# A hybrid decoder layer: block 0's load put into the written order, and a new order for 1200 steps around the change of token halves

## The chip, the core and the metric

The kernel runs on one core of a Trainium2 chip. The core has engines that work side by side, each through its own list of instructions in order: TensorE (PE) multiplies matrices, VectorE (DVE), ScalarE (ACT) and GpSimd (POOL) work element by element, and SyncE (SP) issues the transfers between the chip's memory (DRAM) and the core's on-chip memory. An instruction that waits holds up everything behind it on its engine. The metric is the time of one execution in microseconds (us), the median of several runs.

## The reference

One layer of a hybrid decoder over 2048 tokens of width 1024, in float32. Its first half mixes tokens along two paths (SSD and RWKV7); its second half is a gated feed-forward part with a short causal convolution:

```python
h = x + rms_norm(concat(ssd(xn @ w_in), rwkv7(xn @ w_in)) @ w_out)    # xn = rms_norm(x)
...
u = rms_norm(h) @ w_up                    # 2 x 2816 columns: a gate and a value
u = causal_dwconv(u, conv_w, conv_b)      # 3 taps along the tokens
y = h + rms_norm((silu(gate) * value) @ w_down)
```

## The kernel before, in words

**The whole.** The program has three stages, one after another with some overlap: phase_R (the RWKV path, 16 blocks of 128 tokens), phase_S (the SSD path and the output projection) and phase_F (the feed-forward part). Each float32 operand of a product is split into a high and a low half of 16 bits; the high half is made by ScalarE, the low half ("the value less its high half") by VectorE or GpSimd, and TensorE runs three products of halves instead of one.

**The order of the work.** The order on each engine is written, not found while the program runs. In phase_R a list of words, HEAD, names the steps of the first blocks: `R0.load/5` is step 5 of the load of block 0, `L.w.4/1` is step 1 of loading weight piece 4. A step runs once; a second call of the same step does nothing. HEAD stands under `tc.manual_schedule(engines=HANDS)`, where HANDS are VectorE, ScalarE, GpSimd and SyncE: what is emitted there stays in the order in which it is emitted, while instructions emitted outside are placed by the compiler's scheduler. Block 0's `load` (L845) is emitted ahead of that, at L1399. It reads the 128 token rows (xin), squares them (L870), takes mean and root on GpSimd (L874, L878), scales the rows (L889, ScalarE), makes the high half xh (L890, ScalarE) and the low half (L882, VectorE), has both transposed into xt by transfers (L892, L885), and stores xt in XN (L894). Beside it the weights are loaded: each piece wst (L788, SyncE) is split into wr by ScalarE (L791) and VectorE (L794). The products on L689 need xt and wr.

**The feed-forward part.** It works on two halves of 1024 tokens. In each half there are 22 up products, u_0_0 to u_0_21 and u_1_0 to u_1_21, each computed as seven half-size products (Strassen's scheme) of 12 matmuls, 128x512 outputs each. Their operands are seven combinations b0 to b6 of the tokens, split into halves, and seven combinations w0 to w6 of the weights. The b's of half 1 are built while half 0 ends: token rows hs come from DRAM, GpSimd subtracts (L2026), ScalarE makes the high half (L2051), VectorE or GpSimd the low one (L2056). An up product's results u leave their PSUM banks into C: the first is copied by ScalarE (L2223), the others are added by VectorE (L2227). Then come a scale (L2258), the taps (L2262), silu (L2272) and the gate (L2275), which leave p.

Two up products make a pair, whose p's are combined into seven factors fa (L2315, L2051, L2056). The down products run over two or three pairs: seven combinations dw0 to dw6 of the down weights, split like the b's (L2406, L2409), times fa0 to fa6 (L2445). Their results d are added to acc by ScalarE (L2456) and VectorE (L2458). The names count half, products and quarter: d_0_803 is half 0, the down product after pair 8, and so on.

In half 0 the weights are made on the core and stored in DRAM (UW at L2175, DW at L2414); in half 1 they are loaded back (w at L2147, dw at L2384). The buffers of dw are a ring of four tiles, two for each of dw0 to dw6, so the loads for one step are issued when the products two steps before it are through (dw4 takes the tiles of dw0). The last pair of half 0 (pair 10) is special: its weights are called dwx, in a ring of two tiles that lies where C0 was, and its rows r0, r1 and their difference rt lie where C1 and a1 were. When half 0 ends, Finish adds the norm and the residual and stores the rows (L2494, L2524, L2537, L2544).

**The planner.** phase_F doesn't emit its work at once: each operation is noted with an engine, an estimated time and what it reads and writes, and the class Program (run at L96) puts all of them into one list, todo, by due times worked out back from TensorE's list. The first 140 steps (OPENED) are mixed into the end of phase_S; the rest are emitted one by one under the manual schedule:

```python
todo = prog.run()
yield prog.entry + todo[:OPENED]
prog.on = None
with tc.manual_schedule(engines=HANDS):
    for step in todo[OPENED:]:
        step()
```

Of the kernel before, what the change touches and what calls it, by code (L numbers as in the profile page):

```python
# [389 lines left out]
OPENED = 140  # L390
# [227 lines left out]
""".split())  # L618


HANDS = {getattr(mybir.EngineType, x) for x in ("DVE", "Activation", "Pool", "SP")}


# [70 lines left out]
def phase_R(tc, K, const, tables, x, w_r, w_c, wl_d, g2_d, XN, XC, YR, iters=16):  # L694
    nc = tc.nc
    V, S, G_ = nc.vector, nc.scalar, nc.gpsimd
    with ExitStack() as ctx:
# [696 lines left out]
            return t.rearrange("p j (u s) -> p j u s", s=64)  # L1394

        blocks = [Block(it) for it in range(iters)]
        blocks[0].do("load")
        loads = Loads()
        K.hand.enter_context(tc.manual_schedule(engines=HANDS))  # L1399
        for step in HEAD.split():  # L1400
# [4 lines left out]
        for it in range(2, iters - 1):  # L1405
            for step in PLAN.split():
                step, _, part = step.partition("/")
                who, name, *a = step.split(".")
                n = it + {"n": 1, "f": 0, "b": -1, "a": -2}[who]
# [568 lines left out]
def phase_F(tc, K, w_u, w_d, H, HN, out, halves=2):  # L1978
# [6 lines left out]
    with ExitStack() as ctx:  # L1985
# [607 lines left out]
        for n, h in enumerate(hs):  # L2593
# [25 lines left out]
            if n + 1 < halves:  # L2619
# [2 lines left out]
                ups[n * NFF + NFF].weights()  # L2622
                fin = Finish(n)
        todo = prog.run()
        yield prog.entry + todo[:OPENED]
        prog.on = None
        with tc.manual_schedule(engines=HANDS):
            for step in todo[OPENED:]:
# [5 lines left out]
def hybrid_layer(ctx, tc, io, out):  # L2634
# [8 lines left out]
    with tc.manual_schedule(engines={mybir.EngineType.PE}):  # L2643
        cp = ExitStack()
        const = cp.enter_context(tc.tile_pool(name="const", bufs=1, side="left"))
        tables = [io[n] for n in ("cst", "par", "rows", "rows16")]
        K.hand = ExitStack()
        blocks, front, rest = phase_R(
            tc, K, const, tables, io["x"], io["w_r"], io["w_c"], io["wl"], io["g2"], XN, XC, YR)
        pairs, chunks, setup = phase_S(tc, K, io["x"], io["w_z"], io["w_dt"], io["w_o"], XN, XC, YR, Hd, HN)  # L2650
        F = phase_F(tc, K, io["w_u"], io["w_d"], Hd, HN, out)
        entry = next(F)
        K.hand.close()
# [117 lines left out]
```

## Time and profile before

| | |
|---|---|
| time before, median of 3 runs | 2493.3 us (2490.09 to 2493.72) |
| the profiled execution's own time | 2499.62 us |
| its span, from the first to the last instruction | 2497.8 us |
| granted TensorE clock, mean | 0.986 of full speed |
| busy: TensorE, VectorE, ScalarE, GpSimd | 2398.1, 1909.4, 1197.4, 1082.4 us |

The median comes from unprofiled runs and the rows from one profiled execution, which took 6.3 us more than the median. A row of a timeline gives the start, the duration, the engine, the line in kernel.py, the operation, the tile written and the tiles read, how many instructions the row joins, and in brackets how long the engine had stood idle ahead of it and what released it. PE is TensorE, DVE VectorE, ACT ScalarE, POOL GpSimd, SPq the queue of SyncE. Numbers of buffers are left out there, so `dwx<-r` can be any of the dwx tiles.

### The profile page before, as it was taken

The page shows a single profiled execution, that of the slowest core. Times are in us where ns is not written, and L with a number is a line of the kernel's source. Part 1 is how long each engine was busy: PE and PEld are TensorE (multiplying, and loading weights), DVE is VectorE, ACT ScalarE, POOL GpSimd, SP SyncE. Part 2 cuts the span into 40 slices and gives each one's busy share as a digit, 9 for nine tenths or more (in the row PEclk, how much of TensorE's full clock was granted, in tenths as well). Part 3 has the DMA queues.
Part 4 walks back from the last instruction along what each step waited for, and adds up shares of the span by engine and source line. Part 5 has one row for each costly group of instructions (what it writes and reads, how often), then busy time and mean ns, then how long its engine had stood idle before and what let it go on. Part 6 is the DMA issues. An engine that isn't in the chain of part 4 may idle for free. (4 is left out here: it accounts for less than half of the span.)

```text
span 2497.8 us, 53811 instructions
## 1 busy us (share of the span) xinstructions
PE 2398.1 (96%) x21210; PEld 1519.3 (61%) x21212; DVE 1909.4 (76%) x3790; ACT 1197.4 (48%) x2407; POOL 1082.4 (43%) x1134
## 2 busy tenths in 40 slices
PE   4999999999999899999988999999989999999998
PEld 4899999999999665555533444444434444444443
DVE  6878778877887567678999799999999735546557
ACT  7556665666566544444555545453443432313132
POOL 3334443444344522223334658585847522213135
PEclk9999999999999989999999999999999999999999
DMA  7432332233323536565775444445445533333253
GB/s 224 91 67 58 80 78 67 57 79 75 72 57 71 170 114 170 149 178 162 213 223 166 166 159 147 162 144 177 145 161 192 169 106 97 106 101 98 88 160 109
DMA packets 344412, 319.12 MB, mean 128 GB/s; under 512 B 203232, under 2 KB 248672, under 8 KB 340832
## 3 DMA queue, kind: packets, MB, share of 16 engines
q1 hardware_dynamic: 344016, 315.43, 43.1%
q8 instruction: 166, 2.72, 0.5%
q14 instruction: 86, 0.70, 0.1%
q10 hardware_dynamic: 144, 0.26, 0.0%
HBM read 187.85 MB, written 110.99 MB: 120 GB/s over the span
## 5 line engine op out<-in xcount | busy, mean ns | idle before, releaser
L2205 PE MATMUL u<-b,w 128*128 128x512 f16 x3696 | 809.5, 381 | 22.7 <-ACT C L2223 11.5
L2205 PEld LDWEIGHTS <-w 128*128 128x128 f16 x3696 | 363.2, 98 | 465.1 <-issue 34.5
L689 PE MATMUL d<-xt,wr 128*128 128x129 f16 x5376 | 333.7, 224 | 26.3 <-ACT wr L791 17.9
L689 PEld LDWEIGHTS <-wr 128*128 128x128 f16 x5376 | 319.1, 100 | 40.0 <-ACT wr L791 17.9
L2445 PE MATMUL d<-dw,fa 128*128 128x512 f16 x1512 | 333.6, 380 | 4.2 <-DMA dw<-DW 2.2
L2445 PEld LDWEIGHTS <-fa 128*128 128x128 f16 x1596 | 156.9, 98 | 205.1 <-issue 18.8
L2227 DVE TENSOR_TENSOR C<-u,C 128x512 f32<-128x512 f32 x220 | 150.7, 685 | 156.8 <-PE u L2205 151.3
L689 PE MATMUL c<-xt,wc 128*128 128x131 f16 x3072 | 195.1, 224 | 5.7 <-ACT tv L919 3.5
L689 PEld LDWEIGHTS <-wc 128*128 128x128 f16 x3072 | 183.2, 99 | 11.0 <-issue 7.3
L2458 DVE TENSOR_TENSOR acc<-d,acc 128x512 f32<-128x512 f32 x212 | 140.3, 684 | 54.2 <-PE d L2445 53.3
L2056 POOL TENSOR_TENSOR fa<-p,fa 128x512 f16<-128x512 f32 x100 | 140.7, 1421 | 50.1 <-ACT fa L2051 50.1
L2262 DVE SCALAR_TENSOR_TENSOR p<-C,fpar,p 128x1024 f32<-128x1024 f32 x88 | 124.5, 1415 | 34.5 <-ACT p L2258 34.4
L2058 DVE SCALAR_TENSOR_TENSOR w<-us,w 128x512 f16<-128x512 f32 x132 | 134.3, 1029 | 7.6 <-ACT w L2051 6.6
L968 DVE SCALAR_TENSOR_TENSOR ca<-c,cw,ca 128x128 f32<-128x128 f32 x360 | 114.5, 345 | 25.5 <-ACT ca L958 21.5
L2262 DVE SCALAR_TENSOR_TENSOR a<-C,fpar,a 128x1024 f32<-128x1024 f32 x88 | 125.0, 1420 | 3.7 <-ACT a L2258 2.4
L2223 ACT ACTIVATE C<-u 128x512 f32<-128x512 f32 x88 | 52.2, 593 | 156.9 <-PE u L2205 133.8
L1140 DVE TENSOR_TENSOR tmp<-atl,xl 128x60 f32<-128x60 f32 (+24 forms) x465 | 117.1, 252 | 11.5
L2051 ACT ACTIVATE fa<-p 128x512 f16<-128x512 f32 x110 | 65.4, 623 | 125.0 <-DVE p L2275 113.1
L1146 DVE TENSOR_TENSOR xl<-xl,tmp 128x60 f32<-128x60 f32 (+24 forms) x465 | 111.2, 239 | 13.9
L2051 ACT ACTIVATE w<-us 128x512 f16<-128x512 f32 x132 | 80.3, 624 | 85.6 <-PE u L2205 28.6
L2268 POOL COPY fcarry<-C 128x2 f32<-128x2 f32 x88 | 38.6, 440 | 160.8 <-DVE C L2227 160.7
L2178 POOL TENSOR_TENSOR us<-us,us 128x512 f32<-128x512 f32 x51 | 82.7, 1625 | 46.2 <-DVE w L2058 27.3
(334 smaller groups left out, 4326.3 us busy)
## 6 DMA issues: line engine op xcount, KB each, us to landing
UW<-w SPq DMA_DIRECT2D x154, 256.0 KB
w<-UW SPq DMA_DIRECT2D x154, 256.0 KB
us<-in_w_u_dram SPq DMA_DIRECT2D x88, 256.0 KB
DW<-dw SPq DMA_DIRECT2D x70, 256.0 KB
dw<-DW SPq DMA_DIRECT2D x56, 256.0 KB
hs<-HN SPq DMA_DIRECT2D x48, 256.0 KB
r<-in_w_d_dram SPq DMA_DIRECT2D x10, 1024.0 KB
xin<-in_x_dram SPq DMA_DIRECT2D x16, 512.0 KB
```

Of the source, the lines that this page charges most:

```text
L689: nc.tensor.matmul(ps, w[:, a, kt, :], xt[:, b, kt, cols], start=n == 0, stop=n == 3 * KT - 1)
L968: V.scalar_tensor_tensor(out=acc[:, q], in0=m["rc", e][:, q, k:k + 128], scalar=cw[:, e + q, k:k + 1], in1=acc[:, q], op0=ALU.mult, op1=AL ...
L1140: chain.tensor_tensor(out=self.tmp[:, :k, :n], in0=self.atl[:, j, j + 1:32].unsqueeze(1).to_broadcast([P, k, n]), in1=self.xl[:, :k, j:j + ...
L1146: chain.tensor_tensor(out=self.xl[:, :k, j + 1:32], in0=self.xl[:, :k, j + 1:32], in1=self.tmp[:, :k, :n], op=ALU.add)
L2051: S.activation(h, src, AF.Copy, **({} if scale is None else {"scale": scale}))
L2056: {"V": V, "G": G_}[engine].tensor_tensor(out=l, in0=src, in1=h, op=ALU.subtract)
L2058: V.scalar_tensor_tensor(out=l, in0=src, scalar=scale, in1=h, op0=ALU.mult, op1=ALU.subtract)
L2205: nc.tensor.matmul(bk[at], self.w[i][:, u, k, :], self.half.b[i][:, k, v, :], start=start and n == 0, stop=n == 11, skip_group_check=True)
L2227: op("V", .61, lambda: V.tensor_tensor(out=part(j, x), in0=bk[at], in1=part(*a), op=ALU.add), (("u", 4 * s + at), (*(c0, c1)[a[0]], a[1])) ...
L2262: V.scalar_tensor_tensor(out=o[j], in0=C[j][:, 2 - d:1026 - d], scalar=cw(g, 2 - d), in1=o[j], op0=ALU.mult, op1=ALU.add)
L2445: nc.tensor.matmul(bk[s, t], pairs[m].a[i][:, u, t * P:t * P + P], pairs[m].w[n][0][:, v, :], start=new and m == 0 and u == v == 0, stop=m ...
L2458: V.tensor_tensor(out=acc[j][:, t], in0=bk[s, t], in1=acc[j][:, t], op=ALU.add)
```

## The change

It has two parts. No instruction is added or taken away on any engine.

```diff
@@ -618,6 +618,52 @@
+TURN = 1000
+TURNED = """
+2 30 6 20 1 16 11 15 21 3 0 10 17 5 22 19 8 33 7 9 13 4 14 36 28 18 45 29 27 38 12 32 51 25 23 31 35 43 41 34 47 50 54
...
+1199
+"""
 HANDS = {getattr(mybir.EngineType, x) for x in ("DVE", "Activation", "Pool", "SP")}
@@ -1394,7 +1440,6 @@
         blocks = [Block(it) for it in range(iters)]
-        blocks[0].do("load")
         loads = Loads()
         K.hand.enter_context(tc.manual_schedule(engines=HANDS))
         for step in HEAD.split():
@@ -2622,6 +2667,8 @@
         todo = prog.run()
+        turn = [OPENED + TURN + int(n) for n in TURNED.split()]
+        todo[min(turn):max(turn) + 1] = [todo[n] for n in turn]
         yield prog.entry + todo[:OPENED]
```

First, block 0's load is no longer emitted ahead of the manual schedule. HEAD already names its steps (`R0.load/1` and so on), which until now found the step done; now each is emitted at the place where it stands in HEAD. Second, steps 1140 to 2339 of todo are put into the order of the table TURNED, a permutation of 1200 numbers. A step is moved by 20 places in the mean, by 285 at most. The steps are those of all five engines, so TensorE's order changes as well. On TensorE the stretch runs from u_0_15 of half 0 to u_1_6 of half 1; outside it and the first rows of the front the order on each engine is the same.

In the rows below, the line numbers of the changed kernel are 45 to 47 higher than before's for the same operation.

**At the end of half 0.** ScalarE, around the copy of u_0_210 (the first quarter of the last up product) into C_0_210, before:

```order
L2051 ACTIVATE b0_1_26325<-hs10100_26246 128x512
L2258 ACTIVATE p_0_20_26328<-C_0_200_26165,fpar_21402 128x1024
L2051 ACTIVATE w5_0_21_26348<-us_0_2101_26143 128x512
L2051 ACTIVATE b2_1_26372<-hs10110_26323 128x512
L2223 ACTIVATE C_0_210_26375<-u_0_210_26284 128x512
L2272 ACTIVATE p_0_20_26328<-p_0_20_26328 128x1024
L2051 ACTIVATE fa0_0_10_26399<-p_0_20_26328 128x512
L2223 ACTIVATE C_0_210_26375<-u_0_210_26284 128x512
```

and in the changed kernel:

```order
L2303 ACTIVATE p_0_20_26316<-C_0_200_26123,fpar_21402 128x1024
L2303 ACTIVATE a_0_20_26320<-C_0_201_26124,fpar_21402 128x1024
L2268 ACTIVATE C_0_210_26338<-u_0_210_26232 128x512
L2096 ACTIVATE b0_1_26348<-hs10100_26273 128x512
L2317 ACTIVATE p_0_20_26316<-p_0_20_26316 128x1024
L2096 ACTIVATE w5_0_21_26383<-us_0_2101_26154 128x512
L2096 ACTIVATE b0_1_26348<-hs10300_26277 128x512
L2268 ACTIVATE C_0_210_26338<-u_0_210_26232 128x512
```

The first copy (L2223, now L2268) stood behind the high halves of b0 (from hs10100) and b2 (from hs10110); it now stands ahead of b0, and that of b2 is no longer among these rows.

VectorE, around the low half of the first dwx (from r0, pair 10), before:

```order
L2262 SCALAR_TENSOR_TENSOR a_0_21_26468<-C_0_211_26376,fpar_21402,a_0_21_26468 128x1024
L2409 SCALAR_TENSOR_TENSOR dw4_0_8_26496<-r_0_8_25593,dw4_0_8_26496 128x512
L2275 TENSOR_TENSOR p_0_21_26446<-p_0_21_26446,a_0_21_26468 128x1024
L2409 SCALAR_TENSOR_TENSOR dw4_0_9_26498<-r_0_9_25622,dw4_0_9_26498 128x512
L2315 TENSOR_TENSOR p_0_20_26328<-p_0_20_26328,p_0_21_26446 128x512
L2056 TENSOR_TENSOR fa4_0_10_26517<-p_0_21_26446,fa4_0_10_26517 128x512
L2315 TENSOR_TENSOR p_0_20_26328<-p_0_20_26328 128x512
L2056 TENSOR_TENSOR fa2_0_10_26534<-p_0_20_26328,fa2_0_10_26534 128x512
L2056 TENSOR_TENSOR fa1_0_10_26541<-p_0_20_26328,fa1_0_10_26541 128x512
L2056 TENSOR_TENSOR fa6_0_10_26531<-p_0_21_26446,fa6_0_10_26531 128x512
L2409 SCALAR_TENSOR_TENSOR dwx_0_10_26522<-r0_0_10_26519,dwx_0_10_26522 128x512
```

and in the changed kernel:

```order
L2307 SCALAR_TENSOR_TENSOR a_0_21_26457<-C_0_211_26339,fpar_21402,a_0_21_26457 128x1024
L2101 TENSOR_TENSOR fa0_0_10_26447<-p_0_20_26316,fa0_0_10_26447 128x512
L2307 SCALAR_TENSOR_TENSOR a_0_21_26457<-C_0_211_26339,fpar_21402,a_0_21_26457 128x1024
L2454 SCALAR_TENSOR_TENSOR dwx_0_10_26469<-r0_0_10_26466,dwx_0_10_26469 128x512
L2320 TENSOR_TENSOR p_0_21_26441<-p_0_21_26441,a_0_21_26457 128x1024
L2454 SCALAR_TENSOR_TENSOR dw4_0_8_26471<-r_0_8_25557,dw4_0_8_26471 128x512
L2360 TENSOR_TENSOR p_0_20_26316<-p_0_20_26316,p_0_21_26441 128x512
L2454 SCALAR_TENSOR_TENSOR dw2_0_8_26464<-r_0_8_25557,dw2_0_8_26464 128x512
L2360 TENSOR_TENSOR p_0_20_26316<-p_0_20_26316 128x512
```

The operation on dwx stood behind the gate p_0_21, the combinations p_0_20 and the factors fa4, fa2, fa1 and fa6; it now follows the taps of a_0_21 at once. The factors come later than these rows.

**In the first down product of half 1.** TensorE, from the last bank of dw0 to the first of dw4 (one matmul of each group, the others left out), before:

```order
L2445 MATMUL d_1_003_27799<-dw0_1_0_26902,fa0_1_0_27221 128x512
L2445 MATMUL d_1_003_27799<-dw0_1_1_26932,fa0_1_1_27545 128x512
L2445 MATMUL d_1_010_27809<-dw1_1_0_26968,fa1_1_0_27384 128x512
L2445 MATMUL d_1_010_27809<-dw1_1_1_27001,fa1_1_1_27737 128x512
L2445 MATMUL d_1_000_27760<-dw4_1_0_27816,fa4_1_0_27359 128x512
```

and in the changed kernel:

```order
L2490 MATMUL d_1_003_27693<-dw0_1_0_27113,fa0_1_0_27314 128x512
L2490 MATMUL d_1_003_27693<-dw0_1_1_27342,fa0_1_1_27626 128x512
L2250 MATMUL u_1_42_27524<-b5_1_26476,w5_1_4_27571 128x512
L2250 MATMUL u_1_40_27603<-b4_1_26513,w4_1_4_27568 128x512
L2250 MATMUL u_1_43_27646<-b6_1_26731,w6_1_4_27599 128x512
L2490 MATMUL d_1_011_27771<-dw1_1_0_26922,fa1_1_0_27403 128x512
L2490 MATMUL d_1_001_27684<-dw4_1_0_27794,fa4_1_0_27438 128x512
```

Between the products with dw0 and those with dw1 there now stand three up products of u_1_4, 12 matmuls each.

**At the start of the kernel.** SyncE's queue, around the two transposes into xt_0, before:

```order
L788 DMA wst3_269<-in_w_r_dram 128x4x256
L788 DMA wst4_286<-in_w_r_dram 128x4x256
L788 DMA wst5_289<-in_w_r_dram 128x4x256
L892 DMA_TRANSPOSE xt_0_237<-xh_0_239 128x8x128
L885 DMA_TRANSPOSE xt_0_237<-xin_0_190 128x8x128
L788 DMA wst6_302<-in_w_r_dram 128x4x256
L894 DMA XN0_57<-xt_0_237 2048x1x128
L788 DMA wst7_308<-in_w_r_dram 128x4x256
```

and in the changed kernel:

```order
L834 DMA wst3_265<-in_w_r_dram 128x4x256
L938 DMA_TRANSPOSE xt_0_251<-xh_0_243 128x8x128
L931 DMA_TRANSPOSE xt_0_251<-xin_0_190 128x8x128
L834 DMA wst4_285<-in_w_r_dram 128x4x256
L834 DMA wst5_288<-in_w_r_dram 128x4x256
L834 DMA wst6_301<-in_w_r_dram 128x4x256
L834 DMA wst7_307<-in_w_r_dram 128x4x256
L834 DMA wst8_367<-in_w_r_dram 128x4x256
```

The transposes stood behind the loads of wst4 and wst5 and now stand ahead of them; the store of XN0 stood behind wst6 and has moved further back than these rows. On ScalarE, one split of wst0 now stands ahead of the scaling of the rows and none between it and the high half xh; three stood there before.

41 rows, old and new, of the table TURNED are left out of this document.

## The prediction

> **What bounds the kernel now.** I read the page first: how busy each engine is.
>
> ```profile
> PE 2398.1 (96%) x21210; PEld 1519.3 (61%) x21212; DVE 1909.4 (76%) x3790; ACT 1197.4 (48%) x2407; POOL 1082.4 (43%) x1134
> ```
>
> TensorE works 2398.1 us of a span of 2497.8. The products are the same before and after, so a new order can only win from the 99.7 us in which TensorE stands still, and from time at reduced pace. Next the waits of TensorE (engine, line and awaited instruction: us in total, times, longest) say where it stands.
>
> ```profile
> PE d L689 <- ACT wr L791: 17.9, 1, 17.9
> PE u L2205 <- ACT C L2223: 11.5, 3, 4.9
> PE u L2205 <- DVE C L2227: 8.0, 6, 3.7
> ```
>
> The largest is the start of the kernel, one wait of 17.9 us, which the first part of the change touches. The two below it belong to the feed-forward part. Their places are in the timeline of TensorE around the change of token halves (start, duration, instruction, count, and in brackets the idle time ahead with what ended it).
>
> ```profile
> 1681.86 36.42 PE L2445 MATMUL d<-dw,fa 128*128 128x512 f16 x168
> 1718.12 83.22 PE L2205 MATMUL u<-b,w 128*128 128x512 f16 x384
> 1806.26 9.85 PE L2205 MATMUL u<-b,w 128*128 128x512 f16 x36 [4.92 <-ACT C L2223]
> 1815.95 10.52 PE L2445 MATMUL d<-dw,fa 128*128 128x512 f16 x48
> 1828.39 0.38 PE L2445 MATMUL d<-dwx,fa 128*128 128x512 f16 x1 [1.92 <-ACT dwx L2406]
> 1832.30 5.28 PE L2445 MATMUL d<-dwx,fa 128*128 128x512 f16 x12 [3.54 <-DVE dwx L2409]
> 1839.14 2.53 PE L2445 MATMUL d<-dwx,fa 128*128 128x512 f16 x11 [1.55 <-DVE dwx L2409]
> ...
> 1881.19 13.11 PE L2205 MATMUL u<-b,w 128*128 128x512 f16 x60
> 1895.34 2.75 PE L2205 MATMUL u<-b,w 128*128 128x512 f16 x12 [1.03 <-DVE C L2227]
> 1898.69 75.27 PE L2205 MATMUL u<-b,w 128*128 128x512 f16 x348 [0.60 <-DVE C L2227]
> 1973.80 10.52 PE L2445 MATMUL d<-dw,fa 128*128 128x512 f16 x48
> 1985.42 0.82 PE L2445 MATMUL d<-dw,fa 128*128 128x512 f16 x3 [1.10 <-DMA dw<-DW]
> 1987.33 27.10 PE L2445 MATMUL d<-dw,fa 128*128 128x512 f16 x117 [1.09 <-DMA dw<-DW]
> 2014.27 15.92 PE L2205 MATMUL u<-b,w 128*128 128x512 f16 x73
> ```
>
> The first row is the undisturbed pace: 168 matmuls of the down product in 36.42 us, 0.217 us each, so 2.6 us for a product of 12 and 0.65 us for a bank of 3. From 1718.12 to 2014.27 TensorE has 420 + 252 + 420 + 168 = 1260 matmuls to do, counted from the program; at that pace they take 273 us, and they take 296.15. So about 23 us can be recovered, in four pieces: **A**, the last up products of half 0 (1718.12 to 1815.95, 97.8 against 91), 6.8 us; **B**, the last down product of half 0 (to 1881.19, 65.2 for 252 matmuls against 54.6), 10.6; **C**, the first up products of half 1 (to 1973.80, 92.6 against 91), 1.6; **D**, its first down product (to 2014.27, 40.5 against 36.4), 4.1. Waits are only part of it: in A one wait of 4.92, in B 1.92 + 3.54 + 1.55 = 7.01. The rest is reduced pace: the 12 matmuls after the 3.54 us wait took 5.28 us, twice the pace.
>
> The third view is the busy time by stretch (PE, PEld, DVE, ACT, POOL, then the granted clock, the DMA share and GB/s).
>
> ```profile
> 1816.00:1881.00 65.00, 57.32 (x253) 25.07 (x252) 64.02 (x74) 27.04 (x45) 37.04 (x23) 0.95 0.54 182
> 1881.00:1974.00 93.00, 91.36 (x423) 41.24 (x422) 82.59 (x89) 37.96 (x69) 65.89 (x71) 1.00 0.53 167
> ```
>
> In B VectorE is busy 64.02 us of 65, while TensorE loses 7.68; the granted clock is 0.95 there and 1.00 after. In B VectorE, not TensorE, is the engine without air.
>
> **The change, part by part.** No instruction is added or removed; four places carry the sum.
>
> *A.* What held TensorE for 4.92 us is a copy on ScalarE, and what held the copy stands ahead of it (ScalarE, then GpSimd):
>
> ```profile
> 1805.09 0.63 ACT L2051 ACTIVATE b<-hs 128x512 f16<-128x512 f32 x1 [5.76 <-POOL hs L2026]
> 1805.63 0.58 ACT L2223 ACTIVATE C<-u 128x512 f32<-128x512 f32 x1
> 1826.78 1.59 POOL L2315 TENSOR_TENSOR ft<-p,p 128x512 f32<-128x512 f32 x1 [11.69 <-DVE p L2315]
> ```
>
> ScalarE stood 5.76 us for a GpSimd subtraction (hs) that feeds the high half of b2, and the copy C of u_0_210 came behind. In the new order this copy stands ahead of both b0 and b2. That stall goes, with its stretch at half pace: up to 6.8 us for A.
>
> *B.* The waits are for dwx, the weights of the last pair. VectorE first, then the DMA queue, then VectorE again:
>
> ```profile
> 1826.55 4.03 DVE L2056 TENSOR_TENSOR fa<-p,fa 128x512 f16<-128x512 f32 x3
> 1830.51 1.74 DVE L2409 SCALAR_TENSOR_TENSOR dwx<-r,dwx 128x512 f16<-128x512 f32 x1
> 1823.12 0.32 SPq L2414 DMA_DIRECT2D DW<-dw  x1
> 1823.54 0.38 SPq L2345 DMA_DIRECT2D r<-in_w_d_dram  x1
> 1843.13 0.68 DVE L2409 SCALAR_TENSOR_TENSOR dwx<-r,dwx 128x512 f16<-128x512 f32 x1
> ```
>
> The first dwx (1830.51) stood behind three fa at 4.03 us; the load of r1 (1823.54) behind the store of DW (1823.12); the GpSimd operation at 1826.78, quoted above, had idled 11.69 us for p while the subtractions of r stood behind it. The new order puts dwx from r0 ahead of p, fa4, fa2, fa1 and fa6, the load of r1 ahead of that store, and the subtractions ahead of ft. But TensorE can't gain more than VectorE, which has to finish b1 before the second kind of product of half 1. Here is its end in before:
>
> ```profile
> 1876.57 1.79 DVE L2056 TENSOR_TENSOR b<-hs,b 128x512 f16<-128x512 f32 x1
> ...
> 1878.88 2.83 DVE L2056 TENSOR_TENSOR b<-hs,b 128x512 f16<-128x512 f32 x2
> 1881.63 1.75 DVE L2056 TENSOR_TENSOR b<-ht,b 128x512 f16<-128x512 f32 x1
> 1883.31 0.68 DVE L2458 TENSOR_TENSOR acc<-d,acc 128x512 f32<-128x512 f32 x1
> ```
>
> Ahead of the last b1 (1881.63) the new order leaves out one b3 (1.79) and two b5 (2.83) and takes in one addition to acc (0.68): 3.9 us sooner. VectorE's own idle time in B is 65 - 64.02 = 1.0. And TensorE now runs u_1_02 ahead of u_1_01, one more product of 2.6 that needs no b1. So A and B together give 3.9 + 1.0 + 2.6 = 7.5 us. Ends: 1.0, if only VectorE's idle time goes, and 17.4, if VectorE's work could all wait. I take 7.5, since it is the one value that rests on moved rows.
>
> *C.* The waits 1.03 and 0.60 are for additions of C that stood behind Finish's operations; they now stand ahead of them. 1.6 us, ends 0 and 1.6.
>
> *D.* The load that ended D's second wait, from the chain that ended last:
>
> ```profile
> 1979.97 7.32 DMA dw<-DW
> ```
>
> It takes 7.32 us, is issued when the buffers of dw0 come free, and only dw1's 24 matmuls (5.2 us) cover it. The new order puts three up products of 2.6 between dw0 and dw1: 5.2 + 7.8 = 13 us of cover. Waits of 2.19 go, and 1.9 of reduced pace: 4.1 us, ends 0 and 4.1; I take 4. What then comes last is dw2, loaded when dw1 is free and covered by dw4's 5.2 us; in before it has no wait behind the same cover. The 117 matmuls after the two 1.1 us waits took 27.10 us, 1.7 above pace. [...]
>
> *The front.* The load of block 0 was emitted ahead of the written order and so placed by the scheduler; now its steps stand in HEAD. ScalarE, then the DMA queue:
>
> ```profile
> 8.35 1.29 ACT L791 ACTIVATE wr<-wst,gwr 128x256 f16<-128x256 f32 x3
> 9.54 1.04 ACT L890 ACTIVATE xh<-xin 128x1024 f16<-128x1024 f32 x1
> ...
> 26.05 0.72 ACT L791 ACTIVATE wr<-wst,gwr 128x512 f16<-128x512 f32 x1 [1.73 <-DMA wst<-in_w_r_dram]
> ...
> 10.61 3.41 SPq L892 DMA_TRANSPOSE xt<-xh  x1
> 14.12 2.50 SPq L885 DMA_TRANSPOSE xt<-xin  x1
> ...
> 18.63 0.64 SPq L894 DMA_DIRECT2D XN<-xt  x1
> ```
>
> Three weight splits (1.29 us) stood between the scale and the high copy (9.54); now none, so copy, transposes (10.61) and the first matmul may come up to 1.3 us sooner. The store of XN (18.63) moves behind the next loads, so the 1.73 us wait for wst at 26.05 shrinks. Against it, wst4 and wst5, in before issued ahead of the transposes, now start behind 3.41 + 2.50 us of them, and one of their products is already the last thing awaited:
>
> ```profile
> 25.29 0.23 PE L689 MATMUL d<-xt,wr 128*128 128x129 f16 x1 [1.10 <-DVE wr L794]
> ```
>
> Best 1.3 + 1.7 = 3 us, worst 2 lost (I double the 1.10 of this wait). I take 1 gained.
>
> *New waits.* 1200 steps are permuted by 20 places in the mean, and some wait that no row shows will appear: none at best, 6.2 us at worst (one like the 3.54 with the 2.7 of half pace behind it). I take a third of that, 2.1, since the piled-up waits of before were of 1 to 2 us.
>
> Sum: 7.5 + 1.6 + 4 + 1 - 2.1 = 12.0 us. The profiled execution took 2499.62 us (1.8 around its span), so the changed kernel's would take 2487.6. It was 6.3 above the median of the three runs, 2493.3; the terms are waits inside the span and carry over: 2493.3 - 12.0 = **2481.3 us**. A difference under 0.2% (5 us) can't be told from none.
>
> **The rivals.**
>
> *VectorE holds all.* VectorE's B is fixed work. The same form on L2409 took 0.68 us at 1843.13 and 1.74 at 1830.51, where GpSimd ran beside it; a denser order brings more such overlap, so the 3.9 us may be given back. Then A and B yield 1.0, C nothing, D 4, the front 1, and new waits lie under VectorE's: 2493.3 - 6.0 = 2487.3. For it: 64.02 of 65. Against: the three moved operations really stand behind. Chance 0.2. [...]
>
> *All is recovered.* VectorE's additions to acc wait in PSUM without stopping anything and 23.1 + 1 come back: 2469. Against it is the same row. Chance 0.1.
>
> *Slower: VectorE stops at dwx from r1.* It stood at 1843.13, with five operations between it and dwx from rt; in the new order there are two, and the additions and most of the b's come behind it. VectorE works in order, so if r1 (1 MB) isn't there, everything queued stands, b above all, and TensorE with it. Estimate: VectorE reaches it near 1829 (1843.13 less A's 6.8 and ten operations of 0.7). A load of r1 issued at 1823.54 as now and landing as late as 1841, which the row of 1843.13 allows, would hold VectorE for 12 us. B lost 10.6 for 7.01 of waits, 1.5 for 1, so 12 x 1.5 = 18: 2493.3 - 12 + 18 = 2499.3. It decides from 12 / 1.5 = 8 us of standing still on. Against it: r1's load stands earlier on the queue, and its tile comes free with C1, earlier too. Chance 0.1.
>
> *Nothing to see.* The rows moved are not those that wait last, and the front's two sides cancel: 2493. Chance 0.05.
>
> **How the numbers follow.** My forecast has 0.55. Its own range is 2471 to 2491: A and B at 17.4 and the rest as taken (21.9, 2471.4), or A and B at 1.0 and the front at its worst (2.5, 2490.8). VectorE's case lies inside. I take the range up to 2493 to hold the case of no effect; 2469 and 2499 are the 2 in 10 left out. Faster by over 0.2% (below 2488.3): 0.52 of the forecast, the full recovery's 0.1, half of VectorE's 0.2: 0.72. Within 0.2%: 0.03 + 0.1 + 0.05 = 0.18. Slower: 0.10.
>
> **What would show it.** In the changed profile: no wait for C of ScalarE near 1806; half 1's first product some 7 us earlier against the start of u_0_17, with VectorE still at about 98% ahead of it; no wait for dw from DW in half 1's first down product; the first matmul ahead of 17.5 rather than at 17.91. I am wrong if half 1's first up product starts no earlier, if a wait for dwx of 8 us or more stands there, or if D's load is awaited still.

## The result, and the profile after

| | before | after |
|---|---|---|
| time, median of 5 runs | 2493.3 us (2490.09 to 2493.97) | 2477.94 us (2472.21 to 2481.76) |
| the profiled execution | 2499.62 us, span 2497.8 | 2477.94 us, span 2476.2 |
| granted TensorE clock, mean | 0.986 | 0.991 |

The ratio is 0.9939, with a 95% interval of 0.9923 to 0.9955: 15.4 us less, against 12.0 forecast.

The engines' busy times on the page of the kernel after:

```profile
PE 2386.1 (96%) x21212; PEld 1513.2 (61%) x21212; DVE 1876.3 (76%) x3790; ACT 1193.2 (48%) x2407; POOL 1061.6 (43%) x1134
```

TensorE stands still for 90.1 us of its span (2476.2 - 2386.1) instead of 99.7. More surprising is VectorE: the same 3790 instructions take 33.1 us less (1909.4 before). No term of the prediction's sum had that.

To see where the time went, take the same matmul in both traces and subtract its starts. Up to the end of the front, near 130 us, the difference is -0.1 us; it is still -0.1 at 812 us, then -6.4 at 933 and -6.5 at 1600, and -21.7 behind the stretch, at 2090. So the two profiled executions differ by three pieces: the front 0.1, the SSD stage 6.4, the stretch 15.2. The middle piece is not the change's: the order there is the same. One row for each kernel, of the busy time by stretch, the granted clock being the third number from the end; before:

```profile
810.00:935.00 125.00, 117.15 (x1144) 81.64 (x1142) 76.87 (x181) 59.25 (x141) 49.96 (x94) 0.90 0.45 142
```

and after:

```profile
810.00:935.00 125.00, 117.25 (x1172) 79.37 (x1170) 80.29 (x199) 63.43 (x154) 50.14 (x96) 0.96 0.51 152
```

TensorE is busy for as long, but at a clock of 0.90 against 0.96, with 1144 and 1172 matmuls. This piece comes and goes between executions (in the same window the clock was 0.96 in turn_only, 0.93 in store_late and 0.97 in half1_part, of the experiments below), and before's profiled execution lay 6.3 above its median. The 15.4 us by which the medians differ are about what the stretch gives. That is why the experiments below are read by two numbers: the time, and the change of the difference between about 1573 and 2126 us, called **the stretch's gain**. The gain comes from one profiled execution of each kernel. Each time stands beside runs of before taken with it, whose median moved between 2490.97 and 2493.3 us, so it is the ratios that can be compared.

TensorE in the stretch, after:

```profile
1716.65 75.27 PE L2250 MATMUL u<-b,w 128*128 128x512 f16 x348
...
1810.62 0.38 PE L2490 MATMUL d<-dwx,fa 128*128 128x512 f16 x1 [0.57 <-ACT dwx L2451]
1811.53 1.24 PE L2490 MATMUL d<-dwx,fa 128*128 128x512 f16 x5 [0.53 <-DVE dwx L2454]
...
1818.66 0.38 PE L2490 MATMUL d<-dwx,fa 128*128 128x512 f16 x1 [2.02 <-ACT dwx L2451]
1819.88 2.52 PE L2490 MATMUL d<-dwx,fa 128*128 128x512 f16 x8 [0.83 <-DVE dwx L2454]
1822.18 2.56 PE L2490 MATMUL d<-dw,fa 128*128 128x512 f16 x6
...
1832.58 1.46 PE L2490 MATMUL d<-dw,fa 128*128 128x512 f16 x6 [0.71 <-DVE acc L2503]
...
1834.86 1.46 PE L2490 MATMUL d<-dw,fa 128*128 128x512 f16 x6 [0.18 <-DVE acc L2503]
...
1842.60 1.24 PE L2490 MATMUL d<-dw,fa 128*128 128x512 f16 x5 [1.54 <-DVE dw L2454]
...
1857.92 2.75 PE L2250 MATMUL u<-b,w 128*128 128x512 f16 x12
...
1868.28 80.45 PE L2250 MATMUL u<-b,w 128*128 128x512 f16 x372
1948.57 5.34 PE L2490 MATMUL d<-dw,fa 128*128 128x512 f16 x24
1953.75 7.93 PE L2250 MATMUL u<-b,w 128*128 128x512 f16 x36
1961.52 26.06 PE L2490 MATMUL d<-dw,fa 128*128 128x512 f16 x120
```

A has no wait left, nor have C and D: 372 matmuls run in one row, and D's 120 at the undisturbed pace. All that remains stands in B, seven waits of 6.4 us together. Behind the 2.02 and 0.83 the pace fell as well, at a granted clock of 0.66 from 1820 to 1825: the 8 and 6 matmuls take 2.30 and 2.40 us from start to start, against 1.7 and 1.3 at 0.217 each, 1.7 us more. So about 8 us of the 23.1 stay lost, and 15.2 came back: A 6.8, C 1.6, D 4.1, and 2.7 of B's 10.6. The first product of half 1 starts at 1857.92 instead of 1881.19, with 36 matmuls of half 0 (7.8 us) still behind it.

And the stretch that B now fills, up to that product:

```profile
1804.00:1858.00 54.00, 47.63 (x210) 20.73 (x208) 47.97 (x67) 25.79 (x46) 31.55 (x18) 0.97 0.53 179
```

VectorE is busy for 47.97 of 54 us, 89%, where the prediction wanted to see 98%.

The front, after: TensorE, then ScalarE, then the queue of SyncE.

```profile
14.11 0.27 PE L735 MATMUL d<-xt,wr 128*128 128x129 f16 x1 [14.11 <-DMA xt<-xh]
...
48.10 1.68 PE L735 MATMUL d<-xt,wr 128*128 128x129 f16 x14 [8.70 <-ACT tr L965]
```

```profile
40.70 1.33 ACT L837 ACTIVATE wr<-wst,gwr 128x512 f16<-128x512 f32 x2 [4.26 <-DMA wst<-in_w_r_dram]
```

```profile
10.26 1.35 SPq L938 DMA_TRANSPOSE xt<-xh  x1
11.71 1.36 SPq L931 DMA_TRANSPOSE xt<-xin  x1
...
28.16 0.64 SPq L940 DMA_DIRECT2D XN<-xt  x1
28.97 5.90 SPq L834 DMA_DIRECT2D wst<-in_w_r_dram  x2
```

The first matmul comes 3.8 us sooner (17.91 before). 3.2 of it are the transposes, which stand 1.35 and 1.36 us on SyncE's queue instead of 3.41 and 2.50, with wst4 and wst5 loaded behind them instead of ahead. But it does not last: ScalarE stands 4.26 us for a weight piece whose load is issued behind the store of XN, and TensorE stands 8.70 us behind that. At 48 us 0.3 of the 3.8 is left.

### The profile page after: what moved, and what is told of

Same layout as the page of the kernel before. It is cut to its first block, busy times and chain, and to the rows that moved or that the text cites. A ratio compares the mean times of both kernels' runs of the same rounds, so it can differ in the third digit from the quotient of the medians.

```text
span 2476.2 us, 53715 instructions
## 1 busy us (share of the span) xinstructions
PE 2386.1 (96%) x21212; PEld 1513.2 (61%) x21212; DVE 1876.3 (76%) x3790; ACT 1193.2 (48%) x2407; POOL 1061.6 (43%) x1134
## 4 chain that ended last, share of the span: by engine, by line
PE 40%; DVE 7%; issue 3%; POOL 2%; DMA 2%; ACT 2%; SPq 0%; DVEq 0%; POOLq 0%; ACTq 0%
PE u L2250 25%; PE d L2490 12%; DVE w L2103 1%; PE o L1964 1%; DVE C L2272 1%; PE l L2615 1%; DVE p L2307 1%; DVE a L2307 1%; POOL fa L2101 1%; DMA hs<-HN 0%; PE z L1749 0%; DVE dw L2454 0%; DMA HN<-hT 0%; POOL m L2002 0%; ACT hl L1983 0%
## 5 line engine op out<-in xcount | busy, mean ns | idle before, releaser
L735 PEld LDWEIGHTS <-wr 128*128 128x128 f16 x5376 | 319.9, 100 | 41.2 <-issue 33.1
L2101 POOL TENSOR_TENSOR fa<-p,fa 128x512 f16<-128x512 f32 x100 | 133.6, 1346 | 74.4 <-ACT fa L2096 74.4
L2103 DVE SCALAR_TENSOR_TENSOR w<-us,w 128x512 f16<-128x512 f32 x132 | 127.6, 977 | 9.3 <-ACT w L2096 8.6
L2268 ACT ACTIVATE C<-u 128x512 f32<-128x512 f32 x88 | 52.2, 594 | 169.5 <-PE u L2250 127.2
L2223 POOL TENSOR_TENSOR us<-us,us 128x512 f32<-128x512 f32 x51 | 78.1, 1533 | 50.0 <-DVE w L2103 29.5
L1749 PE MATMUL z<-ws,xs 128*128 128x512 f16 x384 | 92.5, 383 | 0.0
```

The source lines that it names most:

```text
L735: nc.tensor.matmul(ps, w[:, a, kt, :], xt[:, b, kt, cols], start=n == 0, stop=n == 3 * KT - 1)
L2101: {"V": V, "G": G_}[engine].tensor_tensor(out=l, in0=src, in1=h, op=ALU.subtract)
L2103: V.scalar_tensor_tensor(out=l, in0=src, scalar=scale, in1=h, op0=ALU.mult, op1=ALU.subtract)
```

## The experiments

The theory: the two parts of the change are independent, the stretch carries nearly all, and within it half 0's end (A, B) and half 1's start (C, D) each return what their rows say. The rivals: the front carries a share; one moved row does it all; or VectorE's work caps what the two can return together.

**Which part carries it.** front_only is the kernel after without the table, turn_only the kernel after without the change of the front.

```diff
-        turn = [OPENED + TURN + int(n) for n in TURNED.split()]
-        todo[min(turn):max(turn) + 1] = [todo[n] for n in turn]
```

> The changed kernel without the table: block 0's load stands in the written order, the 1200 steps keep their old order. Theory: the earlier start (14.11 against 17.91 us) is given back at the splits of wst10, so by 80 us the two kernels are 0.1 us apart and the time is that of before, 2493.3 within 2 us. Rival (my prediction's front term): 1 us or more is kept, up to 4 us.

```diff
         blocks = [Block(it) for it in range(iters)]
+        blocks[0].do("load")
```

> The table alone; block 0's load is emitted ahead of the manual schedule as before. Theory: all of the gain is the table's, 15 us, so 2478. Rival: the table gives the 11 us of my sum without the front (7.5 + 1.6 + 4 - 2.1), so 2482, and the rest comes from the front.

front_only took 2490.58 us, ratio 0.9993 (0.9982 to 1.0004): not to be told from before. Its stretch, in the old order, has a gain of -0.3. turn_only took 2476.53 us, ratio 0.9941 (0.9929 to 0.9953), with a stretch's gain of 13.8. The table carries the change. The front alone is read best from the same matmul near 129 us: in the six kernels with the new front and the store of XN where the change puts it, it comes 0.1 (after) to 3.4 us (front_only) sooner than before, 1.5 in the mean; in three with the old front 1.0 to 1.1 sooner, and before itself is the zero, 0.8 in the mean. So the front is worth about 0.7 us, less than one execution differs from the next.

**The front's loss.** store_late is the kernel after with the store of XN (R0.load/10 in HEAD) moved behind the issue of the load that was awaited:

```diff
-R0.d.1/5 R0.d.3/3 R0.load/10 R0.d.5/2 R0.scan/4 ...
-R0.d.5/4 L.w.13/0 R0.d.5/5 ...
+R0.d.1/5 R0.d.3/3 R0.d.5/2 R0.scan/4 ...
+R0.d.5/4 L.w.13/0 R0.load/10 R0.d.5/5 ...
```

> The changed kernel with one word of HEAD moved: the store of XN0 (R0.load/10) stands behind the loads of wst10 and wst13 instead of ahead of them. Theory: the store's small pieces, issued at 28.16, hold the load of wst10 (issue 28.97 to 34.32), and ScalarE waits 4.26 us for it at 40.70; without the store ahead most of this goes and 3 to 4 us of the early start are kept: first product with the state at 80 us some 3 us earlier, time 2474 to 2475. Rival: the load of wst10 is held by its own tile or by the load of xin_1 ahead of it, and nothing is won: 2478.

The queue of SyncE and TensorE, in store_late:

```profile
30.05 3.10 SPq L834 DMA_DIRECT2D wst<-in_w_r_dram  x2
33.20 0.64 SPq L940 DMA_DIRECT2D XN<-xt  x1
```

```profile
44.89 1.68 PE L735 MATMUL d<-xt,wr 128*128 128x129 f16 x14 [4.84 <-ACT tr L965]
```

ScalarE's wait for the weight piece is gone, TensorE's wait falls from 8.70 to 4.84 us, and the matmul near 129 us comes 3.8 us ahead of before's. ft_store below has the same edit and repeats both, 4.84 and 3.8. In the six kernels with the store ahead this wait is 5.57 to 8.70 us, and 0.1 to 3.4 us are left. So the store's place on the queue takes part of the front's gain back, 0.4 to 3.7 us by these executions; the 8.70 of after is the worst of them. The time, 2477.98 us, ratio 0.9945 (0.993 to 0.996), does not show it: its stretch gained 13.0 instead of 15.2, and its runs lie between 2471.18 and 2482.18.

**One half of the table at a time.** half0_part keeps the table for the steps below 1923 of todo, which hold half 0's products, and leaves the rest in the old order; half1_part does the reverse; half0_long is half0_part with the cut at 2030, which takes in the first of half 1's steps on all engines as well.

```diff
+        turn = [n for n in turn if n < 1923] + [n for n in range(min(turn), max(turn) + 1) if n >= 1923]
```

> The table for the steps ahead of half 1's first product (step 1923 of the old list) alone; what stands behind keeps its old order. Theory by the two traces: A and B give 9.5 us (23.1 lost before, 7.9 after, of which C's 1.6 and D's 4.1 are not these), so 2478 + 5.7 = 2484, with D's wait for dw back. Rival (my prediction: VectorE's operations ahead of b1 set the start of half 1): 7.5 us or less, 2486 or more.

```diff
+        turn = [n for n in range(min(turn), max(turn) + 1) if n < 1923] + [n for n in turn if n >= 1923]
```

> The counterpart of half0_part: the steps ahead of half 1's first product (step 1923 of the old list) keep their old order, those behind have the table's order; block 0's load is in the written order. half0_part started half 1 some 8.7 us earlier and lost 6.4 of it again at a wait of 5.34 us for VectorE's additions of C, and kept D's waits. Theory: the second part of the table is worth little by itself, C's 1.6 and D's 4.1, so 2493 - 1 - 5.7 = 2486; half 1's first product starts no earlier than in before, and D's wait for dw is gone. The two parts then sum to 8 of the table's 14 to 15 us, the rest is that the first part's gain is kept only with the second. Rival: the parts add up, so this one brings 11 us or more, 2481.

```diff
+        turn = [n for n in turn if n < 2030] + [n for n in range(min(turn), max(turn) + 1) if n >= 2030]
```

> As half0_part, with the cut 107 steps later (2030 instead of 1923): the table's order now also holds for the first additions of C in half 1 and for Finish's first operations among them; D keeps its old order. In half0_part the earlier start of half 1 was lost where the additions of C stood behind Finish's operations and the b's on VectorE (5.34 us). Theory: this piece is what keeps the gain, so from the last down product but one to the second product of half 1 some 9 to 10 us are won instead of 2.3, D's wait for dw stays: 2483. Rival: the loss comes from elsewhere and this adds at most C's 1.6: 4 us won, 2488.

| | time | ratio (95%) | stretch's gain |
|---|---|---|---|
| half0_part | 2487.44 us | 0.9981 (0.9969 to 0.9993) | 2.3 |
| half1_part | 2483.34 us | 0.997 (0.9958 to 0.9981) | 5.8 |
| half0_long | 2486.98 us | 0.9984 (0.9971 to 0.9996) | 4.2 |

half1_part gives what C and D had to lose, 1.6 + 4.1 = 5.7. The two halves' gains don't add up: 2.3 + 5.8 = 8.1, while the whole table gained 15.2, 13.8 and 13.0 in three kernels (after, turn_only, store_late), 14.0 in the mean. The times alone leave that open: the ratios of the two halves make 12 us together and those of the three kernels 14 to 15, each with an interval of about 3 to 4 us either way. Nor does the cut part the table cleanly, since it sends back 13 steps of each side that the table puts on the other. half0_part's trace shows where its gain went. TensorE, in half0_part:

```profile
1865.17 10.09 PE L2250 MATMUL u<-b,w 128*128 128x512 f16 x46
...
1883.96 80.33 PE L2250 MATMUL u<-b,w 128*128 128x512 f16 x360 [5.34 <-DVE C L2272]
...
1975.79 0.82 PE L2490 MATMUL d<-dw,fa 128*128 128x512 f16 x3 [1.15 <-DMA dw<-DW]
1977.70 27.10 PE L2490 MATMUL d<-dw,fa 128*128 128x512 f16 x117 [1.09 <-DMA dw<-DW]
```

and VectorE:

```profile
1866.92 6.79 DVE L2101 TENSOR_TENSOR b<-hs,b 128x512 f16<-128x512 f32 x4
...
1881.56 1.75 DVE L2569 TENSOR_TENSOR acc<-acc,fin 128x512 f32<-128x512 f32 x1
1883.23 0.68 DVE L2272 TENSOR_TENSOR C<-u,C 128x512 f32<-128x512 f32 x1
```

Half 1 starts 8.7 us sooner (16.0 by the two rows, less the 7.3 by which this execution was ahead at 1573), and 5.34 us of it is lost again 19 us later: in the old order VectorE comes to the additions of C only behind the low halves of b at 1.7 us each and Finish's operations. D's waits of 1.15 and 1.09 are untouched. In half0_long the same loss only moves on. TensorE, in half0_long:

```profile
1868.30 44.23 PE L2250 MATMUL u<-b,w 128*128 128x512 f16 x204
1917.08 46.69 PE L2250 MATMUL u<-b,w 128*128 128x512 f16 x204 [4.56 <-ACT C L2268]
```

and VectorE:

```profile
1907.85 3.42 DVE L2582 SCALAR_TENSOR_TENSOR fin<-acc,for,fin 128x512 f32<-128x512 f32 x2 [3.34 <-POOL for L714]
1911.19 0.68 DVE L2272 TENSOR_TENSOR C<-u,C 128x512 f32<-128x512 f32 x1
```

VectorE stood 3.34 us for Finish and did two of its operations before the addition to C; ScalarE's copy came behind, and TensorE waited 4.56 us: half0_long's 4.2 is the 4 of its rival, not the 9 to 10 of its theory. The theory that half 0's share is kept by itself fell in both traces: an earlier start was worth something only as far as the engines behind it were ordered for it too.

**One row at a time.** copy_ahead is the kernel before with three steps of todo turned round, so that the copy of u_0_210 stands ahead of b2's high half, the row that the prediction's A rests on. dw0_ahead is the kernel before with the four banks of dw0 put ahead of three up products, on which D rests.

```diff
         todo = prog.run()
+        todo[1664:1667] = [todo[n] for n in (1666, 1665, 1664)]
```

> The kernel before with two ScalarE steps swapped: the copy of u_0_210 into C_0_210 stands ahead of the high half of b2 (hs10110). Theory: the 4.92 us wait at the end of A goes, and the down product starts 6 to 7 us earlier; but its dwx waits for VectorE's operations, which do not move by as much, so the waits of B grow by about what A gave and half 1 starts at most 2 us earlier: time within 2 us of 2493. Rival: A's 6.8 us are kept to the end, 2486.

```diff
         todo = prog.run()
+        banks = [2194, 2204, 2208, 2211]
+        todo[2171:2212] = [todo[n] for n in banks + [n for n in range(2171, 2212) if n not in banks]]
```

> The kernel before with one thing of the table: the four banks of dw0 of half 1's first down product stand three up products earlier, so that 7.8 us of other work lies between dw0 and dw1. Theory: D's 4.1 us are had by this alone, the waits of 1.1 and 1.1 us for dw and the reduced pace behind them go: 4 us in the stretch, 2489. Rival: the load of dw4 is issued no earlier (the stores of Finish stand ahead of it on SyncE's queue) or another load comes last, and 0 to 1 us is won.

copy_ahead took 2491.23 us, ratio 1.0003 (0.999 to 1.0015), a stretch's gain of 1.3. A's wait fell only from 4.92 to 3.35 us, not to nothing. ScalarE, in copy_ahead, and VectorE:

```profile
1797.61 0.60 ACT L2223 ACTIVATE C<-u 128x512 f32<-128x512 f32 x1 [4.70 <-DVE p L2262]
```

```profile
1791.04 2.29 DVE L2262 SCALAR_TENSOR_TENSOR p<-C,fpar,p 128x1024 f32<-128x1024 f32 x1
...
1795.34 2.17 DVE L2262 SCALAR_TENSOR_TENSOR p<-C,fpar,p 128x1024 f32<-128x1024 f32 x1
```

Behind the wait for GpSimd stood another, for VectorE's taps. So A's 6.8 us are not the work of that one row. In after the copy stands 3.00 us for VectorE's taps as well, but there the table has put banks of the down product between the last up products (the rows left out of the first timeline between 1791 and 1804), and TensorE has those to do meanwhile; that these banks are what hides the rest is argued from the rows.

dw0_ahead took 2490.99 us, ratio 0.9993 (0.9981 to 1.0004). Its D lost 2.5 instead of 4.1: 1.6 came back, and two waits for dw from DW stayed (1.04 and 0.95 us). Its stretch's gain is 1.2. The queue of SyncE, in dw0_ahead:

```profile
1955.72 15.86 SPq L2147 DMA_DIRECT2D w<-UW  x5
1971.67 0.38 SPq L2544 DMA_DIRECT2D out_dram<-fin  x1
1972.11 0.42 SPq L2384 DMA_DIRECT2D dw<-DW  x1
```

and in the kernel after:

```profile
1957.12 14.62 SPq L2429 DMA_DIRECT2D dw<-DW  x5
```

The buffers of dw0 come free sooner in both, but without the table's order on SyncE the load is issued behind five loads of w and a store of Finish: 14.0 us after D's first matmul (1958.12 in its trace), against 8.6 in after (1957.12 less 1948.57). Cover on TensorE alone is not enough; the queue has to come to the load as well.

**What is left in B.** In after, GpSimd takes 4.85 us for one combination (ft from p_0_20 and p_0_21) beside a dense run of VectorE's operations; the load of token rows into p_0_20's tile is issued when it has ended, at 1822.78. GpSimd and the queue of SyncE, after:

```profile
1817.91 4.85 POOL L2360 TENSOR_TENSOR ft<-p,p 128x512 f32<-128x512 f32 x1
```

```profile
1822.78 0.32 SPq L2137 DMA_DIRECT2D hs<-HN  x1
```

Then ScalarE:

```profile
1825.75 0.63 ACT L2096 ACTIVATE b<-hs 128x512 f16<-128x512 f32 x1 [6.62 <-DMA hs<-HN]
```

ft_vector gives this one operation to VectorE; ft_store is ft_vector with store_late's edit.

```diff
+                    g = V if self.extra and not self.half.hf and (o, x) == (nt, n12) else None
-                    op(e, ..., lambda: {"G": either(G_, V), "V": V}[e].tensor_tensor(
+                    op(e, ..., lambda: (g or {"G": either(G_, V), "V": V}[e]).tensor_tensor(
```

> The changed kernel with one operation moved from GpSimd to VectorE: the second ft of pair 10 (p_0_21 less p_0_20). In the changed kernel it took GpSimd 4.85 us beside VectorE, and the load of hs1000 into p_0_20's tile was issued only when it ended (1822.78), with everything on SyncE's queue behind it; b0 waited 6.62 us for it on ScalarE, VectorE then stood 2.38 and 2.93 us, and TensorE waited for acc (0.71 to 3.58 us in three profiles). Theory: on VectorE it takes 0.7 us, the load is issued 3 us or more earlier, the waits for acc go, and the kernel gains 2 to 4 us: 2474 to 2476. Rival: VectorE is the engine without air, one more operation there and nothing is won, 2478 or more.

> ft_vector and store_late together (the store of XN0 behind wst10 and wst13). store_late's profile had no wait for wst10 and stood at the start of d_0_10 at 44.89 us against 46.4 to 48.1 in three profiles with the store ahead. Theory: 1 to 2 us under ft_vector, 2473 to 2475. Rival: nothing beyond ft_vector.

VectorE and ScalarE, in ft_vector:

```profile
1814.09 0.67 DVE L2361 TENSOR_TENSOR ft<-p,p 128x512 f32<-128x512 f32 x1
```

```profile
1820.68 0.63 ACT L2096 ACTIVATE b<-hs 128x512 f16<-128x512 f32 x1 [3.00 <-DMA hs<-HN]
```

What took GpSimd 4.85 us takes VectorE 0.67, ScalarE's wait falls from 6.62 to 3.00, and TensorE no longer waits for acc. The stretch's gain is 17.4 in ft_vector and 17.3 in ft_store, against 14.0 for the table alone. ft_vector took 2475.29 us, ratio 0.994 (0.9928 to 0.9953), which is after's ratio, so its gain is seen in the trace alone. ft_store took 2473.61 us (2470.37 to 2474.62), ratio 0.9924 (0.9911 to 0.9938): the best of all, 17.4 us under the 2490.97 of before beside it. By the traces it beats the kernel after in both places; by the times alone, 0.9924 against 0.9939 with overlapping intervals, that is likely and not shown.

The longest waits left in B have another source. VectorE, GpSimd and ScalarE, after:

```profile
1809.60 1.27 DVE L2307 SCALAR_TENSOR_TENSOR a<-C,fpar,a 128x1024 f32<-128x1024 f32 x1
```

```profile
1814.98 2.97 POOL L2071 TENSOR_TENSOR rt<-r,r 128x512 f32<-128x512 f32 x1 [7.06 <-DMA r<-in_w_d_dram]
```

```profile
1817.98 0.63 ACT L2451 ACTIVATE dwx<-rt 128x512 f16<-128x512 f32 x1 [0.40 <-POOL rt L2071]
```

The rows r1 lie in the ring of C1, whose last reader is this tap of VectorE. It ends at 1810.87, and the load of r1 is issued at 1811.01 (in ft_vector the tap ends at 1808.81, and the subtraction on GpSimd starts at 1812.83, after 6.96 us of standing still). GpSimd stands 7.06 us until it has landed, subtracts in 2.97, and ScalarE's dwx follows, for which TensorE stands 2.02 us. ft, which the table puts behind this subtraction, starts no sooner either. No run here changes the place of that load.

## Why the prediction was right, and where its terms were off

**A and B, 7.5 us, the mis-sized term.** The two gained 9.5, and that is net of the waits that newly stand there, 0.71 and 0.18 for acc and 1.54 for dw; with the 2.1 for new waits the forecast had 5.4. The step that failed is "VectorE, not TensorE, is the engine without air" as a cap: it counted VectorE's operations in B at the durations that they had before. They are not fixed. The low halves of b in the feed-forward part between 1640 and 2040 us, grouped by form, before:

```profile
L2056 DVE TENSOR_TENSOR b<-hs,b 128x512 f16<-128x512 f32 x24 | 27.6, 1168 | 0.0
```

and after:

```profile
L2101 DVE TENSOR_TENSOR b<-hs,b 128x512 f16<-128x512 f32 x24 | 19.5, 832 | 5.3 <-ACT b L2096 5.3
```

The same 24 instructions take 1168 ns each before and 832 after. The fall goes with the table's first part: they take 1147 ns in front_only, which has no table, 850 in turn_only and 827 in half0_long, and the whole kernel's VectorE time is 1909.4 us before and 1876.3 after. What goes with it is GpSimd: of the low halves of b, fa and dw in that window (L2056 and L2409, 66 instructions), the 22 that had no GpSimd operation beside them took 0.67 to 0.70 us each in before, and so did the 27 of after, while those with one beside them all along took 1.30 in the mean before (24) and 0.95 after (20), from 0.68 up to 1.79. VectorE's additions of a product, C<-u,C and acc<-d,acc, which read one operand from PSUM, are a control: all 432 of an execution take 0.67 to 0.70 us, before and after, though in that window GpSimd ran beside 61 of them all along before and beside 80 after. That ordering changes VectorE's time is shown; that it does so through GpSimd alone, and that the 9.5 us come from there, is argued from these rows. The rival "VectorE holds all" looked at the same pair of engines, with the wrong sign: it expected a denser order to bring more overlap, and over the whole execution the two ran at the same time for less, 779.6 us against 828.2. Overlap by itself isn't the measure: of the instructions with a GpSimd operation beside them all along, 5 of 24 before and 12 of 20 after took no longer than those without.

Either engine can be the one that pays. In before GpSimd's ft and r took 1.59 and 1.71 us (1826.78 and 1828.33) and VectorE's three fa beside them 4.03; in after ft took 4.85, and VectorE's operations beside it 0.68 each.

**A's row.** "That stall goes" named one row as the cause, and copy_ahead moved about that row alone: the wait fell from 4.92 to 3.35 us. A's loss did go, but with more of the table than the prediction named.

**C, 1.6, and D, 4.** As measured: no wait for C stands behind Finish in after, D's rows are at the full pace, and half1_part gained 5.8. Of D's reason only half held: "5.2 + 7.8 = 13 us of cover" presumed that the load is issued when its buffer comes free. dw0_ahead has that cover and gets 1.6. The load's place on SyncE's queue is the other half, which the prediction did not name; that D's 4 came out whole is to that extent luck.

D also shows what the pace owes to chance. Behind the same two waits, of 1.00 to 1.15 us, the same 117 matmuls took 27.10 us in before and half0_part, and 25.41 in half0_long:

```profile
1977.05 25.41 PE L2490 MATMUL d<-dw,fa 128*128 128x512 f16 x117 [1.10 <-DMA dw<-DW]
```

At 0.217 us each they are 25.4, so of the 1.9 us of reduced pace in D some belongs to the execution, not to the waits. B shows the same: behind waits of 2.02 and 0.83 us the next 8 matmuls took 2.30 us from start to start in after, at the clock of 0.66, and 1.72 behind the same two waits in half0_part. In these executions waits of 0.8 to 2.0 us cost pace in some cases and not in others.

**The front, 1 us.** About 0.7, but by other terms. The forecast had the first matmul at most 1.3 us sooner and the wait for wst shrinking by the store's move; the first matmul came 3.8 sooner, since the transposes' 3.2 were not counted at all, and the store, though moved back, then stood ahead of a later load, for which ScalarE stood 4.26 us.

**New waits, 2.1.** None outside B; the three in B come to 2.4. **VectorE stops at dwx from r1**, the slower rival, did not come. The queue of SyncE and VectorE, after:

```profile
1811.01 0.33 SPq L2390 DMA_DIRECT2D r<-in_w_d_dram  x1
```

```profile
1820.95 0.68 DVE L2454 SCALAR_TENSOR_TENSOR dwx<-r,dwx 128x512 f16<-128x512 f32 x1
```

The load of r1 is issued at 1811.01 and has landed by 1814.98, when GpSimd starts on it, and VectorE comes to its dwx at 1820.95 without a wait. (It is a load of 512 KB, not of the 1 MB that the prediction gave.) It is GpSimd and ScalarE that the load holds up, as shown above. **All is recovered** stopped about 8 us short, in B. Of the sum's own signs, A's wait, D's load and the first matmul ahead of 17.5 came true; half 1's start was to be "some 7 us" earlier against u_0_17, and by the work done A and B end 9.5 earlier; VectorE "at about 98%" did not hold.

What stays open is the rest of B: the load of r1, the order of r's subtractions on GpSimd and the loads behind them were not taken apart further than ft_vector does.

## What to carry to other kernels

An engine at 98% is a cap only if its instructions cost the same in the new order, and here one form of VectorE's fell from 1168 to 832 ns. Count what an instruction takes alone and beside another engine's (0.67 us and up to 1.79 for VectorE's low halves here) before calling the busier engine the bound. An earlier start is kept only if the engines and the queue behind it are reordered with it, so look for the wait behind the wait: one row moved by itself gained 1.2 to 1.3 us in the stretch where the table gained 14. And a transfer's place on its queue is part of its cost, in both directions: with the store of XN moved behind a load TensorE's wait fell from 8.70 (after) to 4.84 us (store_late), and the load of dw was issued 14.0 us after D's first matmul in dw0_ahead and 8.6 in after.

## What the runs showed of the hardware

- Two transposing transfers stood 3.41 and 2.50 us on SyncE's queue in before, which issues two more weight loads ahead of them, and 1.35 and 1.27 to 1.36 in after, store_late and ft_store, which issue these loads behind them.
- GpSimd's 128x512 operations took 1.15 to 1.28 us at their shortest in the stretch (after, 1780 to 1860) and 4.85 beside a dense run of VectorE's. VectorE's taps, 128x1024, took 1.27 (after) and 2.17 to 2.29 (copy_ahead); its additions of a product, with one operand in PSUM, took 0.67 to 0.70 with GpSimd beside them or not.
- The granted clock in a stage whose order is the same differed between two executions, 0.90 in before and 0.96 in after in the 125 us from 810, and what lies behind that stage came 6.4 us sooner in after.
